# Norm's weights spread over 128 partitions, and k's and v's weights in two halves of the depth: the head of a hybrid decoder block

## The chip, the cores and the metric

The kernel runs on one core of one Trainium2 chip. The metric is the device time of one execution in microseconds. Three runs of the kernel before gave 1584.89, 1586.60 and 1587.22 us; the median is 1586.6 us. The engines are named as the profile names them: PE is TensorE (PEld its weight loads), DVE is VectorE, ACT is ScalarE, POOL is GpSimd, SP is SyncE, whose queue requests most transfers.

## The reference

One layer of a decoder block on x of 1024 positions by 1024 features, all in float32. A norm comes first, and one projection feeds all branches:

```python
h = rms_norm(x, ln1_g[l])
proj = h @ w_in[l] + b_in[l]
rq, rk, rv, rg, aq, ak, av, gate_a, gate_b = jnp.split(proj, SPLIT_IDX, axis=-1)
```

`rms_norm` divides each row of x by its root mean square and multiplies it by the weights `ln1_g`. From the parts the block computes a retention branch, a sliding-window attention branch with 16 query heads and 2 heads of keys and values (`ak` and `av`, 128 columns each, side by side in `w_in`), a gated merge, and then a feed-forward net and a last norm. Only the norm and the products for `ak` and `av` are touched here.

## The kernel before

x is held in eight tiles of 128 positions (`xs`). A float32 operand of a product is split into a high part, a cast to the type that PE takes at full rate, and a low part, the rest; a product is three passes (high by high, low by high, high by low), each of eight steps over the depth of 1024.

The head does this. A small tile of zeros is set (L238), and PE starts 44 warming products of bf16 zeros on it (L264, `WARM1`), so that its clock is up when work arrives. Eight products before the end of these stand two others (L263): a row of ones by the norm's weights, `grow`, which ACT's queue has requested into one partition (L243). Their results, `g`, hold `ln1_g` on all 128 partitions, in two halves of 512 columns. SP requests x tiles 0 and 1, the identity, the weights of k, x tile 2, the weights of v, and the other x tiles (L236 to L251).

ACT squares and sums each x tile (`ln1_stat`, L267), POOL turns the sum into the reciprocal root (L95, L97), DVE multiplies tile, root and `g` in two halves (`ln1_norm`, L209), PE transposes the result in two groups of four (`transpose_hl`, L217), ACT casts the transposed tile to its high part `h` (L222, "the h casts"), and DVE subtracts for the low part (L225). ACT also casts the k weights (L354, two casts of 512 columns, since the columns are reordered for the rotation) and the v weights (L364); POOL (L359) and DVE (L366) make their low parts. For x tiles 0 and 1 this stretch is written in an order that holds for ACT, DVE, PE and POOL; within it PE makes six transposes that only keep it warm (`keep_warm`, L275, `WARM2`).

After that, for each quarter `q` of the positions (two x tiles), PE makes the 24 products of k and the 24 of v (`mm_halves`, L172, 256 columns each); the norms of the next tiles are placed among them by the scheduler, which orders each engine's instructions when the program is built. Every second quarter ends in evacuations (`ak_evac`, `av_evac`). The queries' projection follows from about 45 us, and from about 90 to 330 us the attention units (scores, exponentials, transposes, values; L449 to L505) stand between the dense products of queries and gates, one step of the loop over `NU` units at a time; here too the scheduler sets the order. Then come the retention projections, the merge and the feed-forward net, up to the end.

What the steps of the prediction touch:

```python
grow, ones = wk[0:1, 7, :], wk[0:1, 4, 0:P]
nc.vector.memset(ones, 1.0)
nc.scalar.dma_start(grow, ln1_g)
```

Of the kernel before, what the change touches and what calls it, by code (L numbers as in the profile page):

```python
# [14 lines left out]
ALU = mybir.AluOpType  # L15

P = 128
D = 1024
S = 1024
NB = S // P  # L20
# [1 line left out]
NF = D_FF // P  # L22
EPS = 1e-6
AHEAD = 100
WARM1 = 44
WARM2 = 6
RH = 4
AH = 16
C_RQ, C_RK, C_RV, C_RG, C_AQ, C_AK, C_AV, C_GA, C_GB = (
    0, 512, 1024, 2048, 3072, 4096, 4224, 4352, 5376)  # L30


def f32(t):
    return t.bitcast(F32)
# [3 lines left out]
def hybrid_block(ctx: ExitStack, tc: tile.TileContext, x, ln1_g, w_in, b_in, ret_norm_g, w_ret_out,  # L38
                 attn_sinks, w_attn_out, w_out, ln2_g, w_gate, w_up, w_down, lnf_g,
                 c_ident, c_atab, c_rtab, c_amask, c_rmask, c_rcol, out):  # L40
    nc = tc.nc
    x = x[0]
    out = out[0]
    w_in, w_ret_out, w_attn_out, w_out = w_in[0], w_ret_out[0], w_attn_out[0], w_out[0]
# [72 lines left out]
    def raw_slab(shape, name):  # L117
        return ring.tile([P] + shape, F32, tag="wr", name=f"wr_{name}", bufs=2)

    def hl_tiles(shape, name, pool=None, tag="w"):  # L120
        pool = pool or ring
        return (pool.tile([P] + shape, F32R, tag=tag + "h", name=f"{tag}h_{name}"),
                pool.tile([P] + shape, F32R, tag=tag + "l", name=f"{tag}l_{name}"))
# [88 lines left out]
    def transpose_hl(hx, t, X, banks=(("t", 2), ("t", 2)), wait=None):  # L212
        for q in range(2):
            pt = ps(*banks[q], f"lnT_{q}")
            for i in range(4):
                k = q * 4 + i
                nc.tensor.transpose(pt[:, i * P:(i + 1) * P], hx[:, k * P:(k + 1) * P], ident)  # L217
            v = X[q].rearrange("p (f z) s -> p f z s", z=2)
            ptv = pt.rearrange("p (f s) -> p f s", s=P)
            hi = v[:, :, 0, t * P:(t + 1) * P]  # L220
            lo = v[:, :, 1, t * P:(t + 1) * P]
            nc.scalar.copy(hi, ptv)  # L222

            def rest(lo=lo, ptv=ptv, hi=hi):
                nc.vector.tensor_tensor(out=lo, in0=ptv, in1=f32(hi), op=ALU.subtract)  # L225
            if wait is None:
                rest()
            else:
                wait.append(rest)


    xs = act.tile([P, 8, 1024], F32, tag="B", name="xs")
    wk = act.tile([P, 8, 1024], F32, tag="B", name="wk")
# [4 lines left out]
    nc.vector.memset(wk[:, 5, 0:P // 2], 0.0)  # L238
    warm_w = wk[:, 5, 0:P // 2].bitcast(BF16)

    grow, ones = wk[0:1, 7, :], wk[0:1, 4, 0:P]
    nc.vector.memset(ones, 1.0)
    nc.scalar.dma_start(grow, ln1_g)  # L243
    raws = []
    for t in range(NB):
        if t > 1:
            nc.sync.dma_start(xs[:, t, :], x[t * P:(t + 1) * P, :])
        if 1 <= t <= 2:
            raw = raw_slab([8, P], f"kv{t}")
            c = C_AK if t == 1 else C_AV  # L250
            nc.sync.dma_start(raw, w_in[:, c:c + P].rearrange("(k p) n -> p k n", p=P))  # L251
            raws.append(raw)
    H = [big(A, "A", 0, "h0"), big(A, "A", 1, "h1")]


# [1 line left out]
    warm = acc("warm")  # L257
    with in_order(nc.tensor.engine):
        for n in range(WARM1):
            if n == WARM1 - 8:  # L260
                for q in range(2):
                    gps.append(ps("s", 2, f"g{q}"))
                    nc.tensor.matmul(gps[q], ones, grow[:, q * 512:q * 512 + 512], start=True, stop=True)  # L263
            nc.tensor.matmul(warm[:, 0:P], warm_w, warm_w, start=True, stop=True)  # L264
# [8 lines left out]
    def keep_warm(n):  # L273
        for _ in range(n):
            nc.tensor.transpose(warm[:, 0:P], wk[:, 0, 0:P], ident)  # L275
# [23 lines left out]
    with tc.tile_pool(name="gt", bufs=1, side="right") as gt, tc.tile_pool(name="w1", bufs=1) as w1:  # L299
# [8 lines left out]
            return w1.tile([P, 512], F32, tag=tag, bufs=bufs, name=name)  # L308


        raw = raws[0]
        hi, lo = hl_tiles([8, P], "ak")
        wak = (hi, lo)
        rv_ = raw.rearrange("p k (v z e) -> p k z v e", v=2, z=2, e=32)
        hv = hi.rearrange("p k (z v e) -> p k z v e", z=2, v=2, e=32)
        lv = lo.rearrange("p k (z v e) -> p k z v e", z=2, v=2, e=32)
        def ak_evac(half, pt):
            c = slice(half * 512, half * 512 + 512)
            xb = r512("ra", 2, f"kxb{half}")
# [29 lines left out]
        wav = hl_tiles([8, P], "av")  # L349
        with in_order(nc.scalar.engine, nc.vector.engine, nc.tensor.engine, nc.gpsimd.engine):  # L350
            r01 = [ln1_stat(0), ln1_stat(1)]
            ln1_norm(0, r01[0])
            for z in range(2):
                nc.scalar.copy(hv[:, :, z], rv_[:, :, z])  # L354
            ln1_norm(1, r01[1])
            los = []
            transpose_hl(wk[:, 0, :], 0, H, wait=los)
            for z in range(2):
                nc.gpsimd.tensor_tensor(out=lv[:, :, z], in0=rv_[:, :, z], in1=f32(hv[:, :, z]), op=ALU.subtract)  # L359
            transpose_hl(wk[:, 1, :], 1, H, (("pv", 1), ("acc", 3)), wait=los)  # L360
            keep_warm(WARM2)
            for n in (0, 2, 1, 3):
                los[n]()
            nc.scalar.copy(wav[0], raws[1])  # L364
            r23 = [ln1_stat(2), ln1_stat(3)]
            nc.vector.tensor_tensor(out=wav[1], in0=raws[1], in1=f32(wav[0]), op=ALU.subtract)  # L366
        kb = [acc("ak0"), acc("ak1")]
        vb = [acc("av0"), ps("pv", 1, "av1")]
        for q in range(4):
# [155 lines left out]
        for i in range(NU + 1):  # L525
# [7 lines left out]
            if i > 0:  # L533
                u_values(i - 1)
                if i % 4 == 0:
                    g, b, _, Bt, jb, _ = geo(i - 1)
                    c = slice((b // 4) * 512, (b // 4) * 512 + 512)
# [709 lines left out]
    for nh in range(2):  # L1247
# [4 lines left out]
        for s in range(4):  # L1252
            if s % 2 == 0:
                raws = raw_pair([2, 512], f"wo{nh}{s}")
            raw = raws[s % 2]
# [416 lines left out]
```

## Time and profile before

| what | value |
|---|---|
| median of three runs | 1586.6 us |
| lowest and highest | 1584.89 and 1587.22 us |
| the profiled execution, its own time | 1586.68 us |
| its span, first to last instruction | 1584.9 us |
| PE busy | 1571.2 us, 99% of the span |
| DVE, ACT, POOL busy | 63%, 45%, 23% |
| bytes moved by DMA | 223.13 MB, mean 141 GB/s |

A busy time is the sum of an engine's instructions; PE's ends are modelled, so a busy PE is not PE at its peak. The chain of waits follows the work that ended last back to what released it. The timeline gives an engine's instructions in order of time, neighbours of one kind merged, with the idle time before them and what ended it. The windows give each engine's busy time in a stretch, the clock that TensorE was granted as a share of full speed (PEclk), the busy share of the 16 DMA engines and what they moved.

### The profile page before, as it was taken

Reading aid. Unit: us, or ns where it says so; the run is one execution under the profiler, and the core shown is the slowest. Engines: PE = TensorE matmul, PEld = TensorE weight load, DVE = VectorE, ACT = ScalarE, POOL = GpSimd, SP = SyncE. Lnnn points to the kernel's source line nnn. Section 1 sums busy time; section 2 is a strip of 40 time slices with the busy share of each in tenths; the row PEclk is TensorE's granted clock in tenths of the full one; section 3 lists DMA queues with packets and bytes.
Section 4 is the critical chain, followed back from the end, with each engine's and each line's share of the span. In section 5 each row is a group of like instructions: output and inputs, shape, how many; then the busy total and the mean of one; then the engine's idle time right before and its main releaser. Section 6 shows DMA issues by size and latency. Waiting matters only on the chain.

```text
span 1584.9 us, 20874 instructions
## 1 busy us (share of the span) xinstructions
PE 1571.2 (99%) x7483; PEld 1306.8 (82%) x7483; DVE 996.0 (63%) x1772; ACT 720.9 (45%) x1446; POOL 361.3 (23%) x307
## 2 busy tenths in 40 slices
PE   9999999999999999999999999999999999999998
PEld 8887888888888888888888888888888888788886
DVE  6469978777657663878544368444444444778656
ACT  5258877844233333544221256333333333344445
POOL 2000000000055441000000013555555555200001
PEclk9999999999999999999999999999999999999999
DMA  5564755440364455654545102333333333862233
GB/s 205 156 176 124 204 194 152 140 140 34 128 225 146 133 166 190 230 182 159 176 147 197 54 0 79 102 108 112 106 100 105 108 107 100 306 228 85 99 102 124
DMA packets 148886, 223.13 MB, mean 141 GB/s; under 512 B 9195, under 2 KB 81709, under 8 KB 147246
## 3 DMA queue, kind: packets, MB, share of 16 engines
q1 hardware_dynamic: 148780, 221.79, 43.1%
q8 instruction: 59, 0.97, 0.2%
q14 instruction: 45, 0.37, 0.1%
q10 hardware_dynamic: 2, 0.00, 0.0%
HBM read 149.67 MB, written 67.37 MB: 137 GB/s over the span
## 4 chain that ended last, share of the span: by engine, by line
PE 89%; ACT 6%; DVE 3%; issue 1%; POOL 0%; POOLq 0%; ACTq 0%; DVEq 0%
PE fA L1335 15%; PE fB L1335 8%; PE dA L1596 7%; PE wA L839 7%; PE dxP L1596 6%; PE fC L1335 4%; PE wB L839 3%; PE va L684 3%; ACT sc L464 2%; PE acc_g L155 2%; PE acc_g L156 2%; PE vP L684 2%; PE acc_g L157 2%; PE wo L1275 2%; PE wo L1274 2%; PE acc_ba L156 2%
## 5 line engine op out<-in xcount | busy, mean ns | idle before, releaser
L1596 PE MATMUL dA<-dwP,daP 128*128 128x512 f32 x528 | 121.4, 390 | 0.9 <-DVE xf L1372 0.8
L1596 PEld LDWEIGHTS dA<-dwP,daP 128*128 128x128 f32 x528 | 98.8, 188 | 22.7 <-DVE xf L1372 1.2
L1596 PE MATMUL dxP<-dwP,daP 128*128 128x512 f32 x396 | 90.2, 389 | 0.0
L1596 PEld LDWEIGHTS dxP<-dwP,daP 128*128 128x128 f32 x396 | 74.3, 188 | 15.4
L449 POOL COPY sc<-nsink 128x4 f32<-128x4 f32 x32 | 13.1, 412 | 274.4 <-PE pT L482 152.2
L155 PE MATMUL acc_g<-h,wh_g 128*128 128x512 f32 x192 | 75.5, 393 | 0.1
L1393 POOL TENSOR_TENSOR xf<-xf 128x512 f32<-128x512 f32 x44 | 67.8, 1541 | 32.9 <-issue 30.1
L156 PE MATMUL acc_g<-h,wh_g 128*128 128x512 f32 x192 | 75.3, 392 | 0.0
L157 PE MATMUL acc_g<-h,wl_g 128*128 128x512 f32 x192 | 75.1, 393 | 0.0
L464 ACT ACTIVATE sc<-sc,nm 128x257 f32<-128x257 f32 (+1 forms) x128 | 62.5, 492 | 27.0 <-DVE nm L461 26.6
L1346 POOL TENSOR_TENSOR xf<-xf 128x512 f32<-128x512 f32 x33 | 49.3, 1494 | 54.5 <-ACT t_1P L128 22.4
L461 DVE CUSTOM_DVE_ANT_0 sc<-s,amask,nsink 128x256 f32<-128x256 f32 (+1 forms) x128 | 54.1, 460 | 9.8 <-PE s L458 9.5
L1356 ACT COPY xf<-fA 128x512 f32<-128x512 f32 x44 | 25.8, 588 | 74.3 <-PE fA L1335 74.3
L131 DVE TENSOR_TENSOR dwP<-wd,dwP 128x512 fp32r<-128x512 f32 x77 | 55.9, 727 | 4.6 <-ACT dwP L128 4.6
L128 ACT CAST dwP<-wd 128x512 fp32r<-128x512 f32 x77 | 47.4, 616 | 12.4 <-PE dA L1596 10.0
L155 PE MATMUL acc_bb<-ay,wh_bb 128*128 128x512 f32 x128 | 50.9, 399 | 0.0
L156 PE MATMUL acc_bb<-ay,wh_bb 128*128 128x512 f32 x128 | 50.3, 393 | 0.0
L157 PE MATMUL aq<-h,wl_aq 128*128 128x512 f32 x128 | 50.2, 392 | 0.0
L155 PE MATMUL aq<-h,wh_aq 128*128 128x512 f32 x128 | 50.2, 392 | 0.0
L156 PE MATMUL aq<-h,wh_aq 128*128 128x512 f32 x128 | 50.1, 392 | 0.0
L157 PE MATMUL acc_bb<-ay,wl_bb 128*128 128x512 f32 x128 | 50.0, 391 | 0.0
L1514 POOL TENSOR_TENSOR rs_f<-tot,mhalf 128x1 f32<-128x1 f32 x8 | 4.8, 606 | 198.0 <-DVE tot L1511 198.0
(793 smaller groups left out, 4357.4 us busy)
## 6 DMA issues: line engine op xcount, KB each, us to landing
act_d<-xf SPq DMA_DIRECT2D x77, 256.0 KB, 2.1
daP<-act_d SPq DMA_DIRECT2D x21, 512.0 KB
q_d<-stg SPq DMA_DIRECT2D x8, 1024.0 KB
q<-q_d SPq DMA_DIRECT2D x32, 256.0 KB, 6.6
ay_d<-q SPq DMA_DIRECT2D x8, 1024.0 KB
ay<-ay_d SPq DMA_DIRECT2D x4, 2048.0 KB, 13.2
wr_daP<-act_d SPq DMA_DIRECT2D x14, 512.0 KB, 3.6
wr_g<-in_w_in SPq DMA_DIRECT2D x12, 512.0 KB, 6.3
```

The lines of the kernel that those rows point to most:

```text
L131: nc.vector.tensor_tensor(out=lo, in0=raw, in1=f32(hi), op=ALU.subtract)
L155: nc.tensor.matmul(pt, hi[:, k, :], xh, start=(k == 0), stop=False)
L156: nc.tensor.matmul(pt, hi[:, k, :], xl, start=False, stop=False)
L157: nc.tensor.matmul(pt, lo[:, k, :], xh, start=False, stop=(k == 7))
L461: nc.vector.tensor_tensor_reduce(out=sc[:, j, 0:nk], in0=pt[:, jj * 256:jj * 256 + nk], in1=mk, scale=1.0, scalar=nsink[:, 4 * g + j:4 * g ...
L464: nc.scalar.activation(sc[:, j, 0:nk + 1], sc[:, j, 0:nk + 1], AF.Exp, scale=-1.0, bias=nm[:, j:j + 1], accum_out=den[:, j:j + 1])
L684: nc.tensor.matmul(vbanks[pr][tt], x_[:, c], w[:, u, :], start=(fresh and k + z == 0), stop=(k == 3 and z == 2), skip_group_check=not fresh)
L839: nc.tensor.matmul(pt, o[:, w, k, :], v, start=(first and k + z == 0), stop=(k == 3 and z == 2), skip_group_check=not first)
L1335: nc.tensor.matmul(pt, o[:, w, k, :], v, start=(first and k + z == 0), stop=(k == 3 and z == 2), skip_group_check=not first)
L1346: nc.gpsimd.tensor_tensor(out=dst[q], in0=dst[q], in1=sg[q], op=ALU.mult)
L1393: nc.gpsimd.tensor_tensor(out=o, in0=a, in1=b, op=op)
L1596: nc.tensor.matmul(banks[tt], a[:, u, c], w[:, v, :], start=(fresh and f + z == 0), stop=(f == NP - 1 and z == 2), skip_group_check=not fresh)
```

## The change

Four things change, all in the head:

- `ones` and `grow` cover all 128 partitions. `ones` is zero but for its first row, and `grow` is zeroed by DVE (first half) and POOL (second half) before ACT's queue may request the norm's weights into its first row. The product for `g` has 128 rows, of which 127 are zero.
- Of the 44 warming products 32 are left, and `g` stands ahead of the last four instead of the last eight; `keep_warm` makes two transposes instead of six.
- k's and v's weights are requested together, as two halves of the depth (512 rows by 256 columns each), both ahead of x tile 2. Before, each was one request of 1024 rows by 128 columns, k's ahead of x tile 2 and v's behind it.
- The casts and low parts of k and v are made half by half. For k the second half's casts stand between the h casts of x tiles 0 and 1.

```diff
@@ -22,8 +22,8 @@
 NF = D_FF // P
 EPS = 1e-6
 AHEAD = 100
-WARM1 = 44
-WARM2 = 6
+WARM1 = 32
+WARM2 = 2
 RH = 4
 AH = 16
 C_RQ, C_RK, C_RV, C_RG, C_AQ, C_AK, C_AV, C_GA, C_GB = (
@@ -238,18 +238,19 @@
     nc.vector.memset(wk[:, 5, 0:P // 2], 0.0)
     warm_w = wk[:, 5, 0:P // 2].bitcast(BF16)
 
-    grow, ones = wk[0:1, 7, :], wk[0:1, 4, 0:P]
-    nc.vector.memset(ones, 1.0)
-    nc.scalar.dma_start(grow, ln1_g)
-    raws = []
-    for t in range(NB):
-        if t > 1:
-            nc.sync.dma_start(xs[:, t, :], x[t * P:(t + 1) * P, :])
-        if 1 <= t <= 2:
-            raw = raw_slab([8, P], f"kv{t}")
-            c = C_AK if t == 1 else C_AV
-            nc.sync.dma_start(raw, w_in[:, c:c + P].rearrange("(k p) n -> p k n", p=P))
-            raws.append(raw)
+    grow, ones = wk[:, 7, :], wk[:, 4, 0:P]
+    nc.vector.memset(grow[:, 0:512], 0.0)
+    nc.gpsimd.memset(grow[:, 512:1024], 0.0)
+    nc.vector.memset(ones, 0.0)
+    nc.vector.memset(ones[0:1, :], 1.0)
+    nc.scalar.dma_start(grow[0:1, :], ln1_g)
+
+    assert C_AV == C_AK + P
+    raws = [raw_slab([4, 2 * P], f"kv{i}") for i in range(2)]
+    for i in range(2):
+        nc.sync.dma_start(raws[i], w_in[i * 512:i * 512 + 512, C_AK:C_AK + 2 * P].rearrange("(k p) n -> p k n", p=P))
+    for t in range(2, NB):
+        nc.sync.dma_start(xs[:, t, :], x[t * P:(t + 1) * P, :])
     H = [big(A, "A", 0, "h0"), big(A, "A", 1, "h1")]
 
 
@@ -257,7 +258,7 @@
     warm = acc("warm")
     with in_order(nc.tensor.engine):
         for n in range(WARM1):
-            if n == WARM1 - 8:
+            if n == WARM1 - 4:
                 for q in range(2):
                     gps.append(ps("s", 2, f"g{q}"))
                     nc.tensor.matmul(gps[q], ones, grow[:, q * 512:q * 512 + 512], start=True, stop=True)
@@ -308,12 +309,18 @@
             return w1.tile([P, 512], F32, tag=tag, bufs=bufs, name=name)
 
 
-        raw = raws[0]
-        hi, lo = hl_tiles([8, P], "ak")
-        wak = (hi, lo)
-        rv_ = raw.rearrange("p k (v z e) -> p k z v e", v=2, z=2, e=32)
-        hv = hi.rearrange("p k (z v e) -> p k z v e", z=2, v=2, e=32)
-        lv = lo.rearrange("p k (z v e) -> p k z v e", z=2, v=2, e=32)
+        wak = hl_tiles([8, P], "ak")
+
+        def k_cast(i, low):
+
+            src = raws[i][:, :, 0:P].rearrange("p k (v z e) -> p k z v e", v=2, z=2, e=32)
+            hi, lo = (w[:, 4 * i:4 * i + 4, :].rearrange("p k (z v e) -> p k z v e", z=2, v=2, e=32) for w in wak)
+            for z in range(2):
+                if low:
+                    nc.gpsimd.tensor_tensor(out=lo[:, :, z], in0=src[:, :, z], in1=f32(hi[:, :, z]), op=ALU.subtract)
+                else:
+                    nc.scalar.copy(hi[:, :, z], src[:, :, z])
+
         def ak_evac(half, pt):
             c = slice(half * 512, half * 512 + 512)
             xb = r512("ra", 2, f"kxb{half}")
@@ -350,20 +357,23 @@
         with in_order(nc.scalar.engine, nc.vector.engine, nc.tensor.engine, nc.gpsimd.engine):
             r01 = [ln1_stat(0), ln1_stat(1)]
             ln1_norm(0, r01[0])
-            for z in range(2):
-                nc.scalar.copy(hv[:, :, z], rv_[:, :, z])
+            k_cast(0, False)
             ln1_norm(1, r01[1])
             los = []
             transpose_hl(wk[:, 0, :], 0, H, wait=los)
-            for z in range(2):
-                nc.gpsimd.tensor_tensor(out=lv[:, :, z], in0=rv_[:, :, z], in1=f32(hv[:, :, z]), op=ALU.subtract)
+            k_cast(0, True)
+            k_cast(1, False)
             transpose_hl(wk[:, 1, :], 1, H, (("pv", 1), ("acc", 3)), wait=los)
+            k_cast(1, True)
             keep_warm(WARM2)
             for n in (0, 2, 1, 3):
                 los[n]()
-            nc.scalar.copy(wav[0], raws[1])
+            for i in range(2):
+                nc.scalar.copy(wav[0][:, 4 * i:4 * i + 4, :], raws[i][:, :, P:2 * P])
             r23 = [ln1_stat(2), ln1_stat(3)]
-            nc.vector.tensor_tensor(out=wav[1], in0=raws[1], in1=f32(wav[0]), op=ALU.subtract)
+            for i in range(2):
+                nc.vector.tensor_tensor(out=wav[1][:, 4 * i:4 * i + 4, :], in0=raws[i][:, :, P:2 * P],
+                                        in1=f32(wav[0][:, 4 * i:4 * i + 4, :]), op=ALU.subtract)
         kb = [acc("ak0"), acc("ak1")]
         vb = [acc("av0"), ps("pv", 1, "av1")]
         for q in range(4):
```

ACT, from the squares of x tiles 0 and 1 to the casts of tile 3, as the programs stand (`wr_kv` are the requested weights, `lnT` the transposed tiles in PSUM; line numbers of the change are about ten higher from here on). Before:

```order
L267 ACTIVATE wk,ms<-xs 128x1024 x2
L354 CAST wh_ak<-wr_kv_99 128x8x64 x2
L222 CAST h_109<-lnT_202 128x4x128
L222 CAST h_110<-lnT_208 128x4x128
L222 CAST h_109<-lnT_216 128x4x128
L222 CAST h_110<-lnT_222 128x4x128
L364 CAST wh_av<-wr_kv_102 128x1024
L267 ACTIVATE wk,ms<-xs 128x1024 x3
L222 CAST h_109<-lnT_256 128x4x128
L267 ACTIVATE wk,ms<-xs 128x1024
L222 CAST h_110<-lnT_263 128x4x128
L267 ACTIVATE wk,ms<-xs 128x1024
```

The change:

```order
L268 ACTIVATE wk,ms<-xs 128x1024 x2
L322 CAST wh_ak<-wr_kv_102 128x4x64 x2
L222 CAST h_112<-lnT_193 128x4x128
L222 CAST h_113<-lnT_199 128x4x128
L322 CAST wh_ak<-wr_kv_103 128x4x64 x2
L222 CAST h_112<-lnT_209 128x4x128
L222 CAST h_113<-lnT_215 128x4x128
L372 CAST wh_av<-wr_kv_102 128x512
L372 CAST wh_av<-wr_kv_103 128x512
L268 ACTIVATE wk,ms<-xs 128x1024 x4
L222 CAST h_112<-lnT_249 128x4x128
L222 CAST h_113<-lnT_256 128x4x128
```

k's second half stands after tile 0's two h casts, v's cast is two, and the squares of tiles 2 to 5 all stand ahead of tile 2's h casts; the squares of tiles 6 and 7 follow, and then tile 3's h casts.

PE, around the first k product on x tiles 2 and 3 (`ak` and `av` are the accumulators of k and v, `h` the transposed norm). Before:

```order
L217 MATMUL lnT_272<-ident,wk 128x128 x4
L172 MATMUL av_252<-h_110,wh_av 128x256 x2
L172 MATMUL av_252<-h_109,wl_av 128x256 x4
L172 MATMUL av_252<-h_110,wl_av 128x256 x4
L217 MATMUL lnT_279<-ident,wk 128x128 x4
L172 MATMUL ak_250<-h_109,wh_ak 128x256 x4
L172 MATMUL av_252<-h_109,wh_av 128x256 x4
L172 MATMUL ak_250<-h_110,wh_ak 128x256 x4
```

The change:

```order
L172 MATMUL av_245<-h_112,wl_av 128x256 x4
L172 MATMUL av_245<-h_113,wl_av 128x256 x4
L217 MATMUL lnT_265<-ident,wk 128x128 x4
L217 MATMUL lnT_272<-ident,wk 128x128 x4
L172 MATMUL ak_243<-h_112,wh_ak 128x256 x4
L172 MATMUL av_245<-h_112,wh_av 128x256
L172 MATMUL ak_243<-h_113,wh_ak 128x256 x4
```

Both groups of tile 3's transposes now stand together behind the v products of the quarter before, and one v product instead of four stands between the k products on the first and the second half of the depth.

ACT, early in the attention stage (`sc` are scores and their exponentials, `tb` a gate, `ph` a cast of transposed weights of attention). Before:

```order
L464 ACTIVATE sc_939,den_942<-sc_939,nm_941 128x257
L511 ACTIVATE tb_1234<-acc_g_1_1151,bhalf 128x512
L470 ACTIVATE sc_865<-sc_865,rd_887 128x128 x2
L485 CAST ph_935<-pT_930 128x512
L399 CAST wh_aq_1417<-wr_aq_1421 128x512
```

The change:

```order
L474 ACTIVATE sc_932,den_935<-sc_932,nm_934 128x257 x2
L480 ACTIVATE sc_858<-sc_858,rd_880 128x128 x2
L495 CAST ph_928<-pT_923 128x512
L409 CAST wh_aq_1410<-wr_aq_1414 128x512
L521 ACTIVATE tb_1227<-acc_g_1_1144,bhalf 128x512
```

The gate's evacuation moved behind the scores; such shifts go on up to about 330 us, on PE and DVE too, and from there on the orders are alike.

## Rows read from the trace of the kernel before

**Rows 1.** The page: its head (share of the span, instructions)

```profile
span 1584.9 us, 20874 instructions
...
PE 1571.2 (99%) x7483; PEld 1306.8 (82%) x7483; DVE 996.0 (63%) x1772; ACT 720.9 (45%) x1446; POOL 361.3 (23%) x307
```

**Rows 2.** Chain of waits of the first 45 us: start, us, what

```profile
1.01 4.02 PE warm L264 x36
5.03 3.71 PE g L263 x4
...
9.70 3.43 PE lnT L217 x16
...
13.15 0.59 ACT h L222
...
23.43 1.46 PE ak L172 x10
...
27.90 0.44 PE lnT L217 x4
...
38.82 2.88 PE ak L172 x24
```

**Rows 3.** Timeline of the first 45 us: start, us, engine, line, operation [idle before <-releaser]

```profile
0.72 0.52 ACTq L243 DMA_DIRECT2D wk<-in_ln_g  x1
0.73 0.86 SPq L236 DMA_DIRECT2D xs<-in_x  x2
...
1.27 1.28 ACT L267 ACT_TABLE_LOAD   x1 [1.27 <-PEq L1660]
...
4.39 1.06 ACT L267 ACTIVATE wk<-xs 128x1024 f32<-128x1024 f32 x1 [1.83 <-DMA xs<-in_x]
...
8.65 1.14 ACT L354 CAST wh_ak<-wr_kv 128x512 fp32r<-128x512 f32 x2 [1.88 <-DMA wr_kv<-in_w_in]
...
13.63 1.05 ACT L364 CAST wh_av<-wr_kv 128x1024 fp32r<-128x1024 f32 x1
...
22.79 0.59 ACT L222 CAST h<-lnT 128x512 fp32r<-128x512 f32 x1
...
24.99 0.22 ACT L290 COPY bcol<-bT 128x75 f32<-128x75 f32 x1 [1.61 <-PE bT L289]
```

**Rows 4.** ScalarE's groups, first 24 us: busy, mean ns | idle before <-releasers

```profile
L222 ACT CAST h<-lnT 128x512 fp32r<-128x512 f32 x8 | 4.7, 585 | 2.0 <-PE lnT L217 2.0
```

**Rows 5.** VectorE's groups, first 24 us

```profile
L209 DVE SCALAR_TENSOR_TENSOR wk<-xs,rs_ln,g 128x512 f32<-128x512 f32 x11 | 7.7, 741 | 7.7 <-POOL ve_ln L95 6.2 <-POOL rs_ln L97 0.8 <-PE g L263 0.8
L225 DVE TENSOR_TENSOR h<-lnT,h 128x512 fp32r<-128x512 f32 x8 | 5.3, 687 | 1.5 <-ACT h L222 1.4
...
L238 DVE MEMSET wk<- 128x64 f32 x1 | 0.1, 112 | 0.0
```

**Rows 6.** Windows, whole core: busy of PE, PEld, DVE, ACT, POOL; PEclk, DMA share, GB/s

```profile
5.00:6.50 1.50, 1.50 (x3) 0.78 (x3) 0.00 (x0) 1.42 (x3) 0.79 (x2) 1.00 0.83 239
12.00:15.00 3.00, 3.00 (x22) 3.00 (x21) 2.09 (x4) 2.46 (x5) 0.00 (x0) 1.00 1.02 418
23.50:25.00 1.50, 1.50 (x13) 1.50 (x14) 1.25 (x2) 0.01 (x1) 0.36 (x1) 1.00 1.06 358
```

**Rows 7.** Windows, whole core, up to 11 us

```profile
1.00:8.65 7.65, 7.64 (x40) 4.92 (x40) 0.82 (x2) 3.58 (x6) 1.58 (x4) 1.00 0.86 288
8.65:11.00 2.35, 2.35 (x17) 2.34 (x17) 2.06 (x3) 1.55 (x3) 1.66 (x2) 1.00 1.10 381
```

**Rows 8.** GpSimd's groups, first 24 us

```profile
L359 POOL TENSOR_TENSOR wl_ak<-wr_kv,wh_ak 128x512 fp32r<-128x512 f32 x2 | 2.5, 1282 | 1.6 <-ACT wh_ak L354 1.6
...
L1660 POOL MEMSET const-float32-0.0<- 128x1 f32 x1 | 0.1, 99 | 0.2 <-issue 0.2
```

**Rows 9.** Windows, whole core, attention stage

```profile
100.00:200.00 100.00, 99.19 (x530) 80.35 (x531) 93.77 (x281) 88.32 (x252) 6.64 (x15) 1.00 0.57 167
200.00:300.00 100.00, 97.82 (x520) 81.78 (x519) 79.30 (x233) 78.83 (x218) 5.07 (x13) 1.00 0.53 172
```

## The prediction

> **What bounds the kernel now.** I read the page's head, then the chain of waits of the first 45 us, then each engine's rows there, then busy time by stage. TensorE (PE) is busy 99% of the span [rows 1], so from some 24 us on a microsecond taken from the head should come off the end one for one. The change works in the head, so the question is what PE waits for there.
>
> The chain of the first 45 us [rows 2] is PE alone until 13.15: 36 warming products, the product that spreads the norm's weights (g), eight more warming products (no row shown), 16 transposes. Then ScalarE (ACT) takes over until 23.4. The windows print a granted clock of 1.00 for all of it, but the durations show the lower of the two levels: 36 bf16 products in 4.02 us are 0.112 us for 128 columns (1.2 GHz), and 16 transposes in 3.43 us are 0.214 us each. Later four transposes take 0.44 us, 0.11 us each, and 24 products of 256 columns take 2.88 us, 0.12 us each: 2.4 GHz. So the first 13 us ran at half speed, though PE was never idle after 1.01; the clock rose only after several microseconds of 128-row work that followed g, whose weights fill one row.
>
> What sets the end of the head is ACT. It starts the k weights' cast at 8.65, when they land, and ends the cast of x tile 3 at 22.79 + 0.59 = 23.38 [rows 3], 14.73 us. Of these it idles 2.0 us ahead of the h casts, waiting for transposes [rows 4]; 12.7 us is its own work in a fixed order. PE's k product over tiles 2 and 3 follows at 23.43 [rows 2].
>
> **The change, step by step.**
>
> *Fewer warming products, g earlier.* Ahead of g 28 instead of 36: g starts at 1.01 + 28 x 0.112 = 4.14 instead of 5.03. With rows of zeros it keeps its four pieces of 512 columns, 3.71 us at the low clock: it ends by 7.85 instead of 8.74. Four warming products follow instead of eight, two keeping-warm transposes instead of six.
>
> *The clock.* In the change PE runs 128-row work from 1.01 without the one-row stretch. I expect the clock to be up by the time the transposes start (near 8 us), which makes 16 transposes 16 x 0.11 = 1.8 us of work instead of 3.43. The trace has no g with 128 rows; that it counts as the warming products do is my choice, and the rival below prices the opposite.
>
> *VectorE's norm.* After g's second half (7.85) three pieces of 0.74 us remain [rows 5], done by 10.1; the last four transposes (0.44 us at the high clock) end by 10.6.
>
> *The weights' requests.* Before, k's 512 KB came in pieces of 512 B; now each half holds k and v in pieces of 1 KB. The stretch at 5 us, nearly all k, moved 239 GB/s, that at 23.5 us, 1 KB pieces of the queries' weights, 358, that of x's 4 KB rows 418 [rows 6]. So 524 KB take 2.2 us at the first rate and 1.46 at the second: the first half lands 0.7 us before 8.65, say 8.0. Bounds: no gain (the dip is the queue's and not the pieces') and 0.95 us (the 418 rate). I take 0.65, because the 1 KB row is the same kind of request. The second half lands 1.46 us later, at 9.5; ACT wants it at 8.0 + 0.74 + 2 x 0.55 = 9.85. x tile 2 now stands behind both halves: 2.69 MB, which before were through at about 10 us [rows 7], and its statistics are wanted after v's casts, at about 12.7. So these waits cost nothing.
>
> *ACT's chain in the change.* Two quarter casts of k from 8.0 (2 x 0.37, between the 0.22 of a 75-column copy and the 0.59 of 512 columns [rows 3]), two h casts (L222, 0.55 apart), k's second half (0.74), two h casts ending at about 11.7. Their transposes are done by then (10.6 against 11.15 for the last), so of the 2.0 us of waits I keep 0.2: **-1.8**. The earlier landing: **-0.65**. Three casts more, two for k and one for v: cutting 1.05 us of 1024 columns into two of 0.59 adds 0.13 each [rows 3]: **+0.4**. PE's k product on tiles 2 and 3 can start 2.05 us earlier, near 21.4, but has three v products more left over, by the order shown, 0.12 each: **+0.35**.
>
> *Costs taken at nothing.* The memsets: on VectorE 512 elements lie between the 0.11 of 64 elements and the 0.69 of a two-input operation on 512, on GpSimd between 0.10 and 1.28 [rows 5, 8]. ACT's request for the norm's weights (issued at 0.72, taking 0.52) now waits for them, at the latest until about 2.1, and the activation table (1.28) stands behind it: ready by 3.9, ahead of the first x tile at 4.39 [rows 3]. GpSimd's low parts of k: four pieces at about 0.65, done by 12, wanted a third into the k product at 12.7. SP's queue keeps its order behind the x tiles. Hidden by ACT's wait for x and k; without that cover they would cost at most 1.3 us.
>
> Sum: -1.8 - 0.65 + 0.4 + 0.35 = **-1.7 us**. The profiled execution took 1586.68 us (span 1584.9), 0.1 above the median of 1586.6. Forecast **1585.0 us**, own range 1584.0 to 1586.0. A change of 0.2% is 3.2 us, about the least that a measurement of this kernel tells from none, so the forecast is: no change that can be told.
>
> **Rivals.**
>
> *The clock does not rise before the transposes.* For it: 36 products of 128 rows, 4.02 us, did not raise it in the trace. Against: the change adds nearly 4 us more of them without a break. Then 16 transposes take 3.43 us from about 8.3, the last at 11.75; ACT's fourth h cast slips by 0.6, and the first k products run partly at half speed, hidden behind ACT: 1585.7 us. This is the case in which the change does not do what it says.
> In the trace the clock came up after a stretch in which PE ran only transposes for four microseconds [rows 2]. The Trainium skill, "TensorE: Matmul & The Clock Gate", Part 4 (PE-mode transpose), says the opposite: such transposes do not count as work for the clock. By that rule the keeping-warm transposes do nothing and the sparse transposes of the change leave the clock down, which is this rival's time; by the row, they hold it. The trace disagrees with the rule, so I give this rival 0.15.
>
> *The norm's weights come late* (the side of slower). Place: ACT's request, held until 2.1 and then sharing the engines with x. Before, it is known only to have landed before 5.03. If it took as long as the first x tile (0.73 to 4.39, 3.66 us [rows 3]), it lands at 5.8 and g runs 5.8 to 9.5, 0.8 later than before. With four warming products fewer behind it the transposes, at the low clock, end 0.3 later than before and set ACT's h casts; the landing's gain is lost, k's two casts more fall into waits, v's one and the three v products are paid: 1586.7 + 0.3 + 0.13 + 0.35, **1587.5 us**. It decides once the landing comes after about 5 us. Against: 4 KB is one piece of many. Chance 0.07.
>
> *The attention stage's interleaving gets worse, or better.* From about 90 to 330 us the scheduler places products, scores and transposes differently, as the order shows; the total is the same. PE idles 0.8 us between 100 and 200 and 2.2 between 200 and 300 [rows 9]. Worse: as much again, +3, 1588.1 us, chance 0.09. Better: half of it gone, -1.7 with the head's gain, 1583.3 us, chance 0.15, which also takes the cases in which the head gives more than the sum.
>
> **How the numbers follow.** Forecast 0.54; clock 0.15; late weights 0.07; attention worse 0.09, better 0.15. Below 1583.4 lies two thirds of the better case: faster 0.1. Above 1589.8 a third of the worse one: slower 0.03. Same 0.87. The range reaches from 1583.2 to 1587.6; outside stay part of the better case (0.08) and nearly all of the worse (0.08), under 0.2 together. It holds both ends of the landing (0 and 0.95) and of the waits that remain.
>
> **What would show it.** Transposes L217 before 14 us at 0.11 us each (right) or 0.21 (clock rival). The first k cast at 8.0; at 8.6 the landing term is gone. g at 4.1; near 5.8, the weights were late. ACT's cast of tile 3 ending at 21.4 instead of 23.38. The forecast is wrong if these hold and the time does not fall by 0.7 to 2.7 us: then the stretch from 45 to 359 us took it, to be read as PE idle there.

## The result and the profile after

| | kernel before | changed kernel |
|---|---|---|
| median, 15 runs each on one chip | 1586.54 us | 1589.82 us |
| lowest to highest | 1583.98 to 1587.22 | 1587.61 to 1592.68 |
| profiled execution, its own time | 1586.68 us | 1590.55 us |
| span | 1584.9 us | 1588.8 us |

The ratio is 1.0028, 95% interval 1.0021 to 1.0034: **slower by 3.3 us**, where 1585.0 (1583.2 to 1587.6) was forecast. The times of the kernel before lie in two groups, near 1584.6 and near 1586.6 us, which is why ratios of single versions below have intervals of about 0.09% to either side.

The head of the page of the changed kernel, against [rows 1]:

```profile
span 1588.8 us, 20855 instructions
...
PE 1570.1 (99%) x7467; PEld 1305.0 (82%) x7467; DVE 994.8 (63%) x1775; ACT 721.5 (45%) x1449; POOL 361.3 (23%) x310
```

PE has 16 products fewer and 1.1 us less to do in a span 3.9 us longer: the loss is idle PE, not work. To place it, the two traces are laid side by side at the same instructions (start in us; "pT 21" is the 21st transpose of attention's weights, in order of time):

| first instruction of | before | changed | changed - before |
|---|---|---|---|
| g | 4.96 | 5.87 | +0.91 |
| first transposes (lnT) | 9.49 | 9.34 | -0.15 |
| first k product (ak) | 13.82 | 12.55 | -1.27 |
| transposes of tile 4 | 24.79 | 23.60 | -1.19 |
| queries' products (aq) | 44.41 | 43.63 | -0.78 |
| first scores | 98.79 | 96.20 | -2.59 |
| pT 21 | 120.53 | 117.96 | -2.57 |
| pT 53 | 148.17 | 146.89 | -1.28 |
| pT 85 | 179.02 | 181.49 | +2.47 |
| pT 117 | 203.13 | 207.05 | +3.92 |
| value products of retention (va) | 358.84 | 362.78 | +3.94 |
| end of the span | 1584.90 | 1588.77 | +3.87 |

The head gains as forecast in sign, though half as much. Between pT 21 and pT 117, in the attention stage, 6.5 us are lost; part of this pays back a loan, since the changed order runs 229 products of queries and gates before the first scores instead of 237 (eight of 0.23 us, 1.8). From pT 117 on the difference stays within 0.1 us.

The head, timeline of the changed kernel (start, us, engine, line, operation, [idle before <-releaser]); compare [rows 3]:

```profile
1.58 0.51 ACTq L246 DMA_DIRECT2D wk<-in_ln_g  x1
...
5.87 3.41 PE L264 MATMUL g<-wk 128*128 128x512 f32 x4 [1.70 <-DMA wk<-in_ln_g]
...
8.43 0.71 ACT L322 CAST wh_ak<-wr_kv 128x256 fp32r<-128x256 f32 x2 [1.48 <-DMA wr_kv<-in_w_in]
...
9.34 0.60 PE L217 MATMUL lnT<-ident,wk 128*128 128x128 f32 x4
...
10.13 1.97 PE L217 MATMUL lnT<-ident,wk 128*128 128x128 f32 x12 [0.18 <-DVE wk L209]
...
21.14 1.16 ACT L222 CAST h<-lnT 128x512 fp32r<-128x512 f32 x2
```

Four things are read here. The norm's weights came late: PE waited 1.70 us for them, and g started at 5.87. The clock was up for the transposes (four in 0.60 us, where it took 3.43 us for sixteen before [rows 2]). The first half of k's and v's weights landed at 8.43, 0.22 earlier than k's did before, not 0.65. And the cast of tile 3 ended at 22.30 instead of 23.38.

The attention stage, what PE waited for from 45 to 360 us (us in total, times, longest), of the kernel before:

```profile
PE pT L482 <- ACT sc L470: 1.2, 3, 0.7
PE pT L482 <- DVE sc L472: 0.5, 2, 0.4
PE pT L482 <- ACT tm L500: 0.5, 1, 0.5
PE pv L495 <- DVE tm L502: 0.4, 1, 0.4
PE s L457 <- DVE nm L461: 0.3, 1, 0.3
```

and of the changed kernel:

```profile
PE pT L492 <- ACT sc L480: 1.9, 6, 0.4
PE s L467 <- DVE nm L471: 0.9, 2, 0.6
PE aq L157 <- DVE wl_aq L410: 0.9, 1, 0.9
PE pT L492 <- ACT tm L510: 0.5, 1, 0.5
PE aq L155 <- ACT tb L521: 0.5, 1, 0.5
PE pv L505 <- ACT ph L495: 0.3, 1, 0.3
PE acc_g L157 <- DVE wl_g L131: 0.3, 1, 0.3
PE pv L506 <- DVE pl L496: 0.2, 1, 0.2
```

The lists sum to 2.9 and 5.5 us. New are the waits of products that should fill gaps and need nothing from attention: `aq` for its low halves `wl_aq`, `aq` for an evacuation `tb` that frees its accumulator. They stand at one place. The timeline there, PE and DVE of the changed kernel (a quad is four query heads, whose queries are made together; `stg` is the rotation of the second quad's queries, `wl_aq` the low halves of the third quad's weights):

```profile
117.84 0.69 DVE L427 TENSOR_TENSOR stg<-q,atab 128x512 f32<-128x512 f32 x1
...
121.58 0.39 PE L155 MATMUL aq<-h,wh_aq 128*128 128x512 f32 x1
...
124.67 0.50 PE L155 MATMUL aq<-h,wh_aq 128*128 128x512 f32 x1 [0.48 <-ACT tb L521]
...
126.04 0.39 PE L467 MATMUL s<-kst,q 128*128 128x256 f32 x1 [0.64 <-DVE nm L471]
...
126.94 0.69 DVE L410 TENSOR_TENSOR wl_aq<-wr_aq,wh_aq 128x512 fp32r<-128x512 f32 x1
...
127.68 0.50 PE L157 MATMUL aq<-h,wl_aq 128*128 128x512 f32 x1 [0.90 <-DVE wl_aq L410]
```

The same pair in the kernel before: the low half stands ahead of the rotation, and PE finds it ready:

```profile
116.01 0.69 DVE L400 TENSOR_TENSOR wl_aq<-wr_aq,wh_aq 128x512 fp32r<-128x512 f32 x1
...
120.30 0.68 DVE L417 TENSOR_TENSOR stg<-q,atab 128x512 f32<-128x512 f32 x1
...
121.69 0.39 PE L157 MATMUL aq<-h,wl_aq 128*128 128x512 f32 x1
```

So the changed head made the scheduler write the attention stage in another order. Of the 3.87 us between the profiles a further part is the clock: the trace of the changed kernel records half the granted clock from 128.28 for 3.41 us, right behind these waits; the kernel before has no such record between 13.6 and 1580 us.

### The profile page after: what moved, and what is told of

Read it like the earlier page. It is cut to its first block, busy times and chain, and to the rows that moved or that the text cites. A ratio compares the mean times of both kernels' runs of the same rounds, so it can differ in the third digit from the quotient of the medians.

```text
span 1588.8 us, 20855 instructions
## 1 busy us (share of the span) xinstructions
PE 1570.1 (99%) x7467; PEld 1305.0 (82%) x7467; DVE 994.8 (63%) x1775; ACT 721.5 (45%) x1449; POOL 361.3 (23%) x310
## 4 chain that ended last, share of the span: by engine, by line
PE 89%; ACT 4%; DVE 3%; DMA 1%; issue 1%; POOL 0%; SPq 0%; POOLq 0%; ACTq 0%; DVEq 0%
PE fA L1345 15%; PE fB L1345 8%; PE dA L1606 7%; PE wA L849 7%; PE dxP L1606 6%; PE fC L1345 4%; PE wB L849 3%; PE va L694 3%; PE vP L694 2%; PE acc_g L157 2%; PE acc_g L155 2%; PE acc_g L156 2%; PE wo L1285 2%; PE wo L1284 2%; PE acc_ba L156 2%; PE acc_ba L157 2%
## 5 line engine op out<-in xcount | busy, mean ns | idle before, releaser
L128 ACT CAST dwP<-wd 128x512 fp32r<-128x512 f32 x77 | 47.4, 615 | 12.4 <-PE dA L1606 10.0
L155 PE MATMUL acc_ba<-yg,wh_ba 128*128 128x512 f32 x128 | 49.9, 390 | 0.0
## 6 DMA issues: line engine op xcount, KB each, us to landing
ay<-ay_d SPq DMA_DIRECT2D x4, 2048.0 KB, 13.2
```

The lines of the kernel that those rows point to most:

```text
L155: nc.tensor.matmul(pt, hi[:, k, :], xh, start=(k == 0), stop=False)
```

## The experiments

Theory A: the order of the attention stage costs the time, the head gains a little. The rivals put it in the head's own edits. In the experiments an order is laid on the stretch from the first query products to the end of attention: `impose` chains PE's, DVE's, ACT's and SP's instructions, each engine's in a given order, without a semaphore. Where an expectation below speaks of the "second quad" at 125 us, the third (`quad_q(2)`) is meant.

**Head and order exchanged.** In the first run the head is the changed one and the order that of the kernel before; in the second the other way round.

```diff
+        mark = nc.cur_bb.bb.instructions[-1]
         run(quad_q(0))
...
         fl.rest()
+        impose(tc, nc, mark)
```

> The changed kernel, but from the queries' projection to the end of the attention stage every instruction of PE, DVE, ACT and SP stands in the order of the kernel before. Theory A (the interleaving of the attention stage took the time: its trace loses 4.7 us there, the head gains 0.8): 1585.7 us, 0.8 below the kernel before, no fall of the granted clock near 128 us. Theory B (the head itself costs, by what its requests and its earlier start set off later, in whatever order): 1589.8 us, as the changed kernel. Theory C (the clock fell by a chance of its phase; order and head are innocent): about 1588 us, with a fall in the trace.

> The kernel before, but with the order of the changed kernel from the queries' projection to the end of the attention stage. Theory A: slower by the stage's whole loss, 1586.5 + 4.7 = 1591.2 us, with PE idle between 120 and 135 us. Theory B: 1586.5 us.

Measured: new head, old order 1586.06 us, ratio 1.0000 [0.9991, 1.0008]; old head, new order 1589.55 us, ratio 1.0025 [1.0015, 1.0034]. The order carries the slowdown; the head alone is worth nothing that a measurement tells. The second run misses theory A's 1591.2: its 4.7 us had in them the clock's fall of the one profile, and this run's profile has none in the attention stage.

How it costs is seen in windows between pT 21, pT 53 and pT 85 (busy us and count of PE, PEld, DVE, ACT, POOL; PEclk, DMA share, GB/s). The kernel before:

```profile
120.53:148.17 27.64, 27.10 (x147) 21.89 (x146) 26.32 (x80) 23.81 (x69) 1.06 (x4) 1.00 0.50 153
148.17:179.02 30.85, 30.67 (x162) 24.51 (x160) 30.07 (x81) 26.45 (x74) 3.37 (x4) 1.00 0.58 179
```

Old head, new order:

```profile
117.17:144.68 27.51, 24.82 (x132) 19.09 (x130) 26.04 (x78) 23.45 (x67) 2.73 (x4) 1.00 0.51 154
144.68:179.29 34.61, 34.12 (x176) 27.88 (x177) 29.93 (x80) 26.71 (x72) 1.70 (x4) 1.00 0.51 162
```

The changed kernel:

```profile
117.96:146.89 28.93, 26.28 (x131) 20.59 (x130) 26.18 (x78) 23.52 (x67) 2.34 (x4) 0.94 0.48 147
146.89:181.49 34.60, 34.08 (x177) 27.88 (x177) 29.94 (x80) 26.72 (x72) 1.70 (x4) 1.00 0.52 162
```

The first stretch takes 27.5 to 27.6 us in either order, and DVE is busy for 26.0 to 26.3 of them: it is VectorE that is full there. What differs is how many products PE gets done meanwhile, 147 or 132. Most of these 15 are products of queries and gates (64 begin in that stretch in the kernel before, 51 with the new order). They are made in the next stretch, where PE is the bound (176 products instead of 162; 98 of queries and gates instead of 82, about 0.22 us each): 34.6 us instead of 30.85. Nothing stalls for long: **cheap filler was missing in a stretch that another engine bounds, and was paid for where PE is the bound**. That is read from the windows; no run moved the filler alone. In the changed kernel the first stretch is 1.4 us longer still, with a granted clock of 0.94 in it; the run with the old head has the same order without a fall there, so the fall is an addition and no condition of the loss.

**Each part alone, on the old order.** The halves of k's and v's weights without the new product and warming (the edit shown, in the changed kernel), and the new product and warming alone (its reverse, in the kernel before).

```diff
-WARM1 = 32
-WARM2 = 2
+WARM1 = 44
+WARM2 = 6
...
-    grow, ones = wk[:, 7, :], wk[:, 4, 0:P]
+    grow, ones = wk[0:1, 7, :], wk[0:1, 4, 0:P]
```

> k's and v's weights in two halves alone (one-row product, 44 and 6 warming products as before), attention in the old order. Head alone: the first half lands about 0.2 earlier, three casts more cost 0.4, the transposes still run at half speed: 1586.5 us, between 1586.0 and 1587.0. If the halves carried the head's gain: 1585.7.

> The product over 128 partitions with 32 and 2 warming products alone, k's and v's weights requested as before, attention in the old order. If the earlier clock carries the head's gain (transposes L217 at 0.11 us instead of 0.21): 1585.7 us, with g late as in the changed kernel (near 5.9). If the late norm's weights eat it: 1586.5.

Measured: halves 1585.12 us, ratio 0.9998 [0.9990, 1.0007]; product 1585.76 us, 0.9999 [0.9991, 1.0008]. Neither is told from the kernel before, and the first lies below both of its expectations. In the profiles the queries' products start at 43.98 and 43.68 us, against 44.41 before, 43.90 with both parts and the same order, and 43.63 in the changed kernel: each part brings 0.4 to 0.7, and together they bring no more.

**Each part alone, with the order that the scheduler makes for it.** The same two heads, without `impose`.

> k's and v's halves alone, norm's weights' product and warming as before, attention in the order that the scheduler itself makes (nearly the changed kernel's). Theory A (the halves move the scheduler's order, the order costs time): slower, 1588.3 to 1589.8, PE's waits for wl_aq and tb near 125 us as in the changed kernel, unit 8 to unit 12 in 34.6 us instead of 30.85. Rival B (the slowdown needs the late weights of norm, which shift the phase in which attention starts): 1586, within 0.05% of before.

> The product over 128 partitions and the 32/2 warming alone, requests and casts as before, attention in the scheduler's own order, which lies near that of before (the low halves of the second quad stand ahead of the rotation). Theory A: the same as before within 0.7 us, 1585.6 to 1586.8, no wait for wl_aq. Rival B (any edit of the head that moves the order costs some us): 1588 or more.

Measured: halves 1589.67 us, ratio 1.0028 [1.0018, 1.0038]; product 1585.26 us, 0.9996 [0.9988, 1.0005]. The same halves cost 0.28% with one order and nothing with another, and pT 53 to pT 85 takes 34.62 us in the first, where PE waits 0.9 us for `wl_aq` as expected but not for `tb`. **It was the requests' halves that tipped the order**; the product leaves it good (146 products between pT 21 and pT 53, the next stretch 30.75 us). The first run's rival B, that the late weights of norm are needed for it, falls, and so does the second's, that any edit which moves the order costs.

**One engine's order alone.** The changed kernel; only PE's, then only DVE's order is that of the kernel before, and the scheduler fits the others to it.

```diff
+ORDERS = {
+    "PE": "0+3 -24+3 4+19 ...",
+}
...
+        impose(tc, nc, mark)
```

The dots inside the list stand for the rest of PE's row; in the second run the list is DVE's.

> The whole change, in attention TensorE's order alone that of before; the other engines' orders follow by the scheduler and put the second quad's first low half still earlier. Theory A1 (what costs is that TensorE's row has the next quad's products ahead of what VectorE has done, and any order in which the two fit is as good): 1586.0 to 1586.9. Rival A2 (VectorE's and ScalarE's rows have to be those of before as well): 1587.5 to 1589.5.

> The whole change, in attention VectorE's order alone that of before, TensorE's and ScalarE's orders follow by the scheduler. Theory A1 (the two rows have to fit): 1586.0 to 1587.0, the wait for wl_aq near 125 us gone. Rival A2 (TensorE's row itself has to be that of before): 1587.5 to 1589.5.

Measured: PE's alone 1595.34 us, ratio 1.0063 [1.0050, 1.0075]; DVE's alone 1587.27 us, 1.0009 [1.0000, 1.0018]. For PE's row both theories miss, and by far. With PE's old row and the DVE row that the scheduler makes to it, one value product waits 3.4 us for a low part, which is a part of the 8 us between the profiles' spans (scores wait 2.9 us near 170 us, and the clock falls twice, see the last section); what PE waited for from 115 to 130 us:

```profile
PE pv L532 <- DVE pl L522: 3.4, 1, 3.4
```

With DVE's old row the wait for `wl_aq` is gone, as A1 said, but the time stays 0.3 us above A1's upper end, and 153 products fill a first stretch of 29.40 us. So neither row is good or bad by itself: the runs fit the reading that what counts is how the rows fit together, and with all four as before the loss is nil.

**One instruction moved.** In the changed kernel with its own order, the first low half (126.94 us above) goes ahead of the rotation; in the kernel before, the same low half goes back behind five operations of the rotation. The fence sketches the two moves (in the program one number moves in DVE's list).

```diff
 DVE, changed kernel:
+    wl_aq (quad 2, first half)
     stg x5 ...
-    wl_aq (quad 2, first half)
...
 DVE, kernel before:
-    wl_aq (quad 2, first half)
     ...
     stg x5
+    wl_aq (quad 2, first half)
```

> The changed kernel with its own orders, one VectorE instruction moved: the first low half of the third quad's query weights (wl_aq, at 126.9 us in the profile of the changed kernel) stands ahead of the rotation's first operation, where the kernel before has it. Theory C (the slowdown is this row: PE's q products wait for the low halves at the quad's boundary): the wait of 0.9 us goes and the later low halves come 0.6 us sooner, 0.9 to 1.5 us less, 2.3 to 2.9 where the clock no longer falls near 128 us: 1587.0 to 1588.9. Rival D (the waits of a whole new interleaving, of which this is one; the next wait takes its place): 1589.3 to 1590.3.

> The kernel before with its own orders, the same low half moved back behind five of the rotation's operations, where it ends near 124.0 us; PE wants it at 121.7 us. Theory C: PE stalls some 2.3 us there and nothing gives it back: 1.5 to 2.5 us above before in the same runs, and wl_aq heads PE's waits of that stretch. Rival E (work further on takes it up, since PE has slack in attention): less than 0.7 us above before.

Measured: earlier 1589.90 us, ratio 1.0030 [1.0019, 1.0042], no gain; later 1588.16 us, 1.0015 [1.0006, 1.0024], slower, by 2.4 us from the ratio and by 2.0 between the profiles' spans. The second is as theory C has it, by PE's waits from 115 to 130 us:

```profile
PE aq L186 <- DVE wl_aq L429: 2.2, 1, 2.2
```

In the first the wait for `wl_aq` is gone and others have taken its place (from 45 to 360 us; 5.7 us in all, as in the run with the old head and the new order):

```profile
PE pT L521 <- ACT sc L509: 1.7, 6, 0.4
PE s L496 <- DVE nm L500: 1.5, 2, 1.2
PE pT L521 <- DVE sc L511: 0.8, 1, 0.8
```

So rival D holds for the changed kernel: in the order of before one late low half is enough to cost 2.2 us, but putting it right in the new order does not give the loss back. PE still has 132 products between pT 21 and pT 53 there, in 27.92 us, and the next stretch takes 34.61; that PE's own row, which was left as it was, keeps them out is argued from this.

**The norm's weights early.** The whole change, with the request issued first, into row 0 of a free slice, and a copy by DVE after the memsets; the order is that of the kernel before, then that of the product alone.

```diff
     grow, ones = wk[:, 7, :], wk[:, 4, 0:P]
+    nc.scalar.dma_start(wk[0:1, 3, :], ln1_g)
...
-    nc.scalar.dma_start(grow[0:1, :], ln1_g)
+    nc.vector.tensor_copy(out=grow[0:1, :], in_=wk[0:1, 3, :])
```

> The whole change with attention in the order of before; norm's weights are requested ahead of everything into row 0 of a free slice, as before at 0.7 us, and copied into row 0 of the cleared rows by VectorE. Theory F (the late packet cost the head some 0.9 us): g's products start near 4.2 us instead of 5.87, the first transposes come some 0.9 us sooner than in the run with the new head and the old order, and the whole is 0.3 to 1.0 us less than that run: 1584.3 to 1585.8. Rival G (the first norm waits for something else by then, the square or the x tile): the transposes move by less than 0.3 us and the time is that run's, 1585.7 to 1586.6.

> As the run with early weights, but attention in the order that the scheduler made for the product alone, whose stretch from the first query product to the last of attention took 313.65 us instead of 314.43. Theory F: 0.5 to 1.0 us less than with the order of before: 1583.7 to 1585.2. Rival H (that difference was within what two profiles of one order differ by): the same as with the order of before within 0.3 us.

Measured: 1584.65 us, ratio 0.9997 [0.9988, 1.0006], and 1584.10 us, 0.9993 [0.9984, 1.0002]. Both lie well below the changed kernel and neither is told from the kernel before. g starts at 3.97 us in both. What that is worth is seen against a profile with late weights whose clock rose just as early (4.26 and 4.32 us), the run with one cast earlier (timelines of the head). With the weights early and the old order:

```profile
3.97 2.08 PE L294 MATMUL g<-wk 128*128 128x512 f32 x4
...
7.25 2.72 PE L246 MATMUL lnT<-ident,wk 128*128 128x128 f32 x16 [0.97 <-DVE wk L238]
...
8.55 0.71 ACT L352 CAST wh_ak<-wr_kv 128x256 fp32r<-128x256 f32 x2 [1.70 <-DMA wr_kv<-in_w_in]
...
9.17 1.06 ACT L251 CAST h<-lnT 128x512 fp32r<-128x512 f32 x2
...
11.38 1.23 PE L201 MATMUL ak<-h,wh_ak 128*128 128x256 f32 x8 [1.19 <-ACT h L251]
```

With the weights late:

```profile
5.88 1.95 PE L293 MATMUL g<-wk 128*128 128x512 f32 x4 [1.70 <-DMA wk<-in_ln_g]
...
8.01 2.64 PE L246 MATMUL lnT<-ident,wk 128*128 128x128 f32 x16
...
8.48 0.71 ACT L351 CAST wh_ak<-wr_kv 128x256 fp32r<-128x256 f32 x2 [1.45 <-DMA wr_kv<-in_w_in]
...
9.10 1.06 ACT L251 CAST h<-lnT 128x512 fp32r<-128x512 f32 x2
...
11.31 1.23 PE L201 MATMUL ak<-h,wh_ak 128*128 128x256 f32 x8 [0.45 <-ACT h L251]
```

The transposes come 0.76 us sooner (theory F's first half), the first k product 0.07 us later: ACT has the k cast ahead of the h casts in its row, and that cast waits for the weights' first half either way. By 42 us nothing is left of it (the queries' products start at 42.45 and 42.38). So with an early clock and these weights landing at 8.5, early weights of norm are no gain; with a late clock, where ACT waits 0.84 us for the first transposes in the changed kernel, no such pair was run. That late ones are no part of the slowdown is shown by the runs that have them and the old order or the product's own: 1586.06, 1585.76 and 1585.26 us. Theory F's times hold, and the transposes move by more than rival G allows, but this pair shows no gain that F's reason would account for. The profile of the run with the new head and the old order has its clock up at 9.4, the two with early weights at 4.3 and 6.0; that the clock makes the difference is argued from one profile each. Rival H or F for the other order: 1584.10 against 1584.65, both inside each other's interval, and the profiles take 313.54 and 314.27 us from the first query product to the first of retention, the same 0.7 us as between the product alone and the kernel before. Not settled by the times.

## Why the prediction was wrong

*The step that failed* is that the sum has no term for the attention stage: it lets a microsecond of the head "come off the end one for one" and leaves the reordered stage to a rival ("the total is the same") with a chance of 0.09, for which no row is given. In its place the runs showed that the order alone costs 3.3 us from the first query product to pT 117 in the profile with the old head, and 3.0 between the medians; the changed kernel's profile lost 4.7 there, 1.4 of it by the clock's fall, of which nothing was said. The rival's price, "as much again, +3", was nearly right, but it is PE's idle time taken twice and not read from the orders, so that is luck. What would show the forecast wrong was named rightly: idle PE between 45 and 359 us. The order of the changed program held a hint: it has the third quad's first low half behind the rotation, and in the trace of the kernel before PE takes that half at 121.69, while each operation of the rotation takes 0.6 us of a DVE that is 95% busy there. The price was not to be had from this place alone, since moving the low half forward gave nothing back; laying the whole new row on the old durations was not tried.

*The clock* came out as forecast in the changed kernel's profile. It was up by 8.8 us, the first four transposes took 0.60 us, and the rival by which it does not rise before them falls there. In two of the nine profiles with the new warming (the product alone on the old order, and PE's old row) it rose at 10.4, some 0.6 us after the first transposes had begun, and in four at 4.3 to 6.0. Against the Trainium skill, "TensorE: Matmul & The Clock Gate", Part 4 (PE-mode transpose), which does not count such transposes as work for the clock, stand two further profiles with the old head (the halves alone on the old order, and one cast later): their clock rose at 12.7 and 13.2 us, while PE had run nothing but transposes since 9.5; the trace disagrees with the rule there. In the changed kernel the rise falls into g itself, so that profile says nothing on it.

*The norm's weights* were the rival with 0.07, and it happened: g at 5.87, forecast 4.14, the rival's 5.8. Its price was wrong. It took the transposes at the low clock; with the clock up they ended at 12.1, before those of the kernel before, and with an early clock the last runs show that ACT's wait for k hides what remains.

*The landing*, -0.65 for the first half at 8.0: it came at 8.43, -0.22. The bound "no gain" was the nearer one. *ACT's h waits*, -1.8: the 2.0 us [rows 4] became 1.1 in the first 24 us, -0.9. The page of groups for that stretch:

```profile
L222 ACT CAST h<-lnT 128x512 fp32r<-128x512 f32 x8 | 4.5, 586 | 1.1 <-PE lnT L217 1.1
```

*The memsets* (0.52 and 0.48 us) were hidden as such, as said; what they cost is that they held the norm's request back until 1.58. *Three casts more*, +0.4: ACT works 12.78 us from 8.43 to 22.30, against 12.71 from 8.65 to 23.38 before, so this term was 0.07. *The sum*: tile 3's cast ended at 22.30 instead of 21.4, 1.08 earlier than before. The k product that [rows 2] shows at 23.43 is not the first on tiles 2 and 3, as the prediction reads it, but the one on the second half of the depth. The first half's, before:

```profile
21.91 0.73 PE L172 MATMUL ak<-h,wh_ak 128*128 128x256 f32 x4
```

Both halves' in the changed kernel:

```profile
21.77 0.74 PE L172 MATMUL ak<-h,wh_ak 128*128 128x256 f32 x4
...
22.46 0.65 PE L172 MATMUL ak<-h,wh_ak 128*128 128x256 f32 x4
```

So the second half's product, which needs tile 3's last cast, came 0.97 earlier, the first half's 0.14. Of the second's gain 0.78 was left at 44 us, and with the old order (the run with the new head) 0.51 there and 0.1 at the end of the span, 0.35 of it lost near 285 us, where PE waits 0.9 instead of 0.5 us for a softmax of ACT. So a microsecond of the head did not come off the end one for one: in these profiles attention took part of it back even with an unchanged order.

## What to carry to other kernels

A change in one stage of a scheduled program can rewrite the order of a later one; before costing it, compare the orders over the whole program, and where they differ look at stretches that a second engine binds: count the products that each order places there (147 against 132 here) and, with the old trace's times, whether what they need is ready. To judge an edit apart from the order it provokes, run it with the old order laid on; here that turned +0.28% into nothing. And look at what stands ahead of a small request: here 4 KB that memsets held back by 0.86 us landed 3.6 us later than before (5.73 against 2.10), behind the x tiles that had been requested in the meantime.

## What the runs showed of the hardware

- One 4 KB request on ACT's queue, issued at 1.58 us behind the first x tiles on SP's, was under way for 4.15 us by the chain of waits of the changed kernel. Its one packet of data ran from 5.22 to 5.38, just as the last of the 256 packets of x tiles 0 and 1 began (5.29); in the seven profiles with the late request it began at 5.14 to 5.29. Issued at 0.72, ahead of them, it had landed by 2.1 us in the kernel before and by 2.5 with the early request.
- The granted clock in the head differs between executions. In six of the fourteen profiles it rose at 4.2 to 6.0 us, in the others at 8.7 to 13.6. With the old warming and the one-row g it rose at 12.7 to 13.6 in three profiles, and in the two where it rose early it fell again 3.4 us later and was back near 11 to 12; with the new warming and the 128-row g it rose by 10.4 in all nine and did not fall again in the head. With the new warming the first k product came at 11.3 to 11.4 us after an early rise, at 12.4 to 12.9 after a late one. In the profiles whose attention stage has the order of before or the product's own, the execution took 1584.1 to 1584.6 us after an early rise (three) and 1586.6 to 1586.7 after a late one (four, the kernel before among them): 2 us, two thirds of what the order costs. Their heads differ, and no profile of the kernel before has an early clock, so that the rise makes these 2 us is argued, not shown.
- In the changed kernel the clock fell to half for 3.41 us near 128 us, after three waits of 0.48 to 0.90 us within 4 us; with the halves alone and their own order it fell at 127.1 us, while the profile with the old head and the same order, which has the same three waits (0.50, 0.60 and 0.90 us), and that with one cast moved show none. With PE's old row it fell at 123.1 and 170.9, 0.4 us after waits of 3.4 and 2.9 us had ended. What decides it was not tried.
- Which of the scheduler's estimates the halves tipped was not tried either.
